# Hybrid block on one core: the weights' second parts made by ScalarE and an accumulating DMA, used last in each block, and three other jobs moved off GpSimd

## The chip, the core and the metric

The kernel runs on one core of a Trainium2 chip. The metric is the device time of one execution in microseconds (us). Three runs of the kernel before gave 914.47, 915.35 and 921.18 us; the median, 915.35 us, is the time that the change is compared with.

## The reference: what is computed

One layer over 512 tokens of width 1024, all in float32:

```python
h = rmsnorm(x, attn_norm_g)
proj = h @ w_in                                   # 1024 x 5408
p_sb, p_rw, p_gate = jnp.split(proj, ...)
# A: stick-breaking attention, 8 heads of 64, swept in blocks of 128 queries
# B: RWKV-7 time mixing, 8 heads of 64: state update over 512 steps, group norm, bonus, gate
gates = jax.nn.sigmoid(p_gate + branch_gate_b)
x = x + (sum over branches of gates * (branch @ w_branch)) @ w_out
u_gate, u_val = causal_depthwise_conv(rmsnorm(x) @ w_ffn_up)   # 1024 x 5632
x = x + (silu(u_gate) * u_val) @ w_ffn_down                    # 2816 x 1024
```

## The kernel before

Everything is kept transposed: channels on the 128 partitions, the 512 tokens along the free dimension. A dense product is cut into **blocks** of 128 output channels. Each operand of a block is split into two parts of a shorter format: `hi` is the rounded value, and `lo` is what the rounding left over. A block of 1024 input channels is then 8 k-steps of three matmuls, 24 in all: `hi` of the weight with `hi` of the activation (line 127), `hi` of the weight with `lo` of the activation (line 128), and `lo` of the weight with `hi` of the activation (line 129).

The weight of a block goes through four steps, in `load_w` and `load_w2`: SP's queue issues the load of `wraw` (512 KB); ScalarE (ACT) rounds it to `whi`; a subtraction `wraw - whi` gives `wlo`, in two halves of four k-steps each; TensorE (PE) uses both. `wraw` and `whi` have two buffers, `wlo` four halves, so two blocks are in hand. The subtraction is on VectorE (DVE), but while `state["pool"]` is set, which is in the whole first phase, it is on GpSimd (POOL).

The program has two phases. In **phase 1** (to about 450 us) PE serves several streams at once: `dense_stream` makes the projection's blocks (tiles `pd`), four `rw_stream`s make the RWKV branch (tiles `pr`), four `att_stream`s the attention (tiles `pz`, `po`). `interleave` merges them: each stream yields what its matmuls cost, or how long it has to wait, and a table of latencies (`LAT`) says how far ahead dense work is put. That order is fixed when the program is built; the order on the other engines is set by a list scheduler, and every engine then works strictly in its own order. In **phase 2** (gates, branches, output, feed-forward) there are dense blocks alone, on tiles `pf`; there the subtraction is on DVE before and after the change.

In phase 1 the dense stream calls `load_w(..., half=True)` for the next block when it starts a block: that issues the load, the rounding, and the first half of `wlo`. The second half follows after the fourth k-step of the running block.

Of the other streams three places matter. `rw_stream` prepares for each pair of heads the tiles `ARV` and `BK`: the values are copied into `ARV` by POOL (line 435), and each of the two products that fill `BK` (lines 448 and 453) is made half by DVE and half by POOL. The next step (line 456, DVE) overwrites an input of the second product, so it waits for POOL's half. `L517` and `L519` are the 31 steps of a triangular solve, two short DVE instructions each. `att_stream` makes for each piece of scores a softmax-like chain: three ACT steps on `e`, one on DVE (line 701), a split into `sph` (ACT, line 121) and `spl` (DVE, line 122), two matmuls into `pz`, two ACT steps for `w`, and a DVE step `wtl` (line 733); POOL keeps the running sums (`e`, `ach`, `acl`, lines 709 to 712).

Of the kernel before, what the change touches and what calls it, by code (L numbers as in the profile page):

```python
# [12 lines left out]
ALU = mybir.AluOpType  # L13
# [3 lines left out]
P = 128  # L17
D = 1024
T = 512
KT = D // P  # L20
# [32 lines left out]
def hybrid_block(ctx: ExitStack, tc: tile.TileContext, xT, w_in, vecs, decay_up, iclr_up, out_gate_up,  # L53
                 w_branch, w_out, w_up, w_down, out):
    nc = tc.nc
    V, A, G, PE = nc.vector, nc.scalar, nc.gpsimd, nc.tensor
# [3 lines left out]
    state = {"load": None, "members": [], "funcs": ()}  # L60
# [17 lines left out]
    def f(ap):  # L78
        return ap.bitcast(F32)
# [16 lines left out]
        return vec[:, o : o + w] if o < NVEC1 else state["vec2"][:, o - NVEC1 : o - NVEC1 + w]  # L96


    def load_w(src, nk, half=False):


        raw = wpool.tile([P, KT, P], F32, tag="wraw", name="wraw")
        nc.sync.dma_start(raw[:, 0:nk], src.rearrange("(k p) c -> p k c", p=P))
        hi = wpool.tile([P, KT, P], F32R, tag="whi", name="whi")
        A.copy(hi[:, 0:nk], raw[:, 0:nk])  # L105
        w = (hi, [], raw)
        for _ in range(1 if half or nk <= 4 else 2):
            load_w2(w, nk)
        return w

    def load_w2(w, nk=KT):
        hi, los, raw = w
        k0 = 4 * len(los)
        n = min(4, nk - k0)
        lo = wpool.tile([P, 4, P], F32R, tag="wlo", name="wlo", bufs=4)
        (G if state.get("pool") else V).tensor_tensor(lo[:, 0:n], raw[:, k0 : k0 + n], f(hi[:, k0 : k0 + n]),  # L116
                                                      op=ALU.subtract)
        los.append(lo)

    def split(hi, lo, src):  # L120
# [3 lines left out]
    def mm1(ps, w, k, act, first, last):  # L124

        (ah, al), hi, lo = act, w[0][:, k], w[1][k // 4][:, k % 4]
        PE.matmul(ps, hi, ah, start=first, stop=False)  # L127
        PE.matmul(ps, hi, al, start=False, stop=False)  # L128
        PE.matmul(ps, lo, ah, start=False, stop=last)  # L129
# [11 lines left out]
    h_acts = [(hhi[:, k], hlo[:, k]) for k in range(KT)]  # L141
# [32 lines left out]
    gl1 = cpool.tile([96, T], F32R, name="gl1")  # L174
# [18 lines left out]
    with tc.tile_pool(name="p0", bufs=1) as p0, \  # L193
# [39 lines left out]
        for k in range(KT):  # L233
# [6 lines left out]
                PE.matmul(ps, w[1][k // 4][:, k % 4], hhi[:, k], start=False, stop=False)  # L240
            for ps, w in (pl0, w0), (pk0, w1):
                PE.matmul(ps, w[0][:, k], hlo[:, k], start=False, stop=(k == KT - 1))
        state["pool"] = True
        mu1 = cpool.tile([P, 15], F32, name="mu1")
        V.tensor_scalar(mu1, vcol("mu", 0, 15), -1.0, 1.0, op0=ALU.mult, op1=ALU.add)
        ndb = cpool.tile([P, 8], F32, name="ndb")
# [10 lines left out]
        for j in range(2):  # L257
            hr = slice(64 * j, 64 * j + 64)
# [76 lines left out]
    def c3(a):  # L335
        return a.rearrange("p (c t) -> p c t", t=CH)
# [43 lines left out]
    def rw_stream(p):  # L380
        d = RD[p]
# [6 lines left out]
        for j, bn in ((0, "db"), (1, "ib")):  # L388
            pl = rbank()
            PE.matmul(pl, lup[j][:, p * P : (p + 1) * P], wl2[j], start=True, stop=False)  # L390
            hr = slice(64 * j, 64 * j + 64)
# [40 lines left out]
        r = d["r"]  # L432
        ARV = rwp.tile([P, NC, 3, CH], F32, tag="ARV", name="ARV", bufs=2)
        for h, (hr, _) in enumerate(HROWS):
            G.tensor_copy(ARV[hr, :, 2 - h, :], c3(d["v"])[hr])
        BK = rwp.tile([P, NC, 2, CH], F32, tag="BK", name="BK", bufs=1)
        Rp = ARV[:, :, 0, :]
        act(c, c, AF.Exp, scale=GAM)
# [4 lines left out]
        for h, (hr, _) in enumerate(HROWS):  # L443
            V.scalar_tensor_tensor(ARV[hr, :, 1 + h, :], c3(kk)[hr], -1.0, c3(c)[hr], op0=ALU.mult, op1=ALU.mult)
        V.tensor_tensor(kk, kk, ic, op=ALU.mult)
        for E, h in (V, 0), (G, 1):
            hr = HROWS[h][0]
            E.tensor_tensor(BK[hr, :, h, :], c3(kk)[hr], e3[hr], op=ALU.mult)
        V.tensor_scalar(ic, ic, vcol("keya", p), ka1[:, p : p + 1], op0=ALU.mult, op1=ALU.add)
        V.tensor_tensor(k, k, ic, op=ALU.mult)  # L450
        for E, h in (V, 0), (G, 1):
            hr = HROWS[h][0]
            E.tensor_tensor(BK[hr, :, 1 - h, :], c3(k)[hr], e3[hr], op=ALU.mult)
        V.tensor_tensor(Rp, Rp, c3(r), op=ALU.mult)

        V.scalar_tensor_tensor(k, r, vcol("rk", p), k, op0=ALU.mult, op1=ALU.mult)
# [330 lines left out]
    def load_gl(c0):  # L787

        raw = wpool.tile([P, KT, P], F32, tag="wraw", name="wraw")
        nc.sync.dma_start(raw[:, :, 0:32], w_in[:, c0 : c0 + 32].rearrange("(k p) c -> p k c", p=P))  # L790
        hi = wpool.tile([P, KT, P], F32R, tag="whi", name="whi")
        A.copy(hi[:, :, 0:32], raw[:, :, 0:32])
        G.tensor_tensor(hi[:, :, 32:64], raw[:, :, 0:32], f(hi[:, :, 0:32]), op=ALU.subtract)
        return hi, None, raw

    def dense_stream():
# [27 lines left out]
        while cur:  # L824
            c0, evac, args, name, gate_ev = cur
            for e in gate_ev:
                yield ("after", e)
            yield ("after", f"bank{i - 2}")
            w, cur = nxt, pick()
            if cur:  # L830
                nxt = load_gl(cur[0]) if cur[3] == "gl1" else load_w(w_in[:, cur[0] : cur[0] + P], KT, half=True)
            ps = bank()
            for k in range(KT):
                if name == "gl1":
                    PE.matmul(ps[0:64], w[0][:, k, 0:64], hhi[:, k], start=(k == 0), stop=False, skip_group_check=True)
                    PE.matmul(ps[0:32], w[0][:, k, 0:32], hlo[:, k], start=False, stop=(k == KT - 1),
                              skip_group_check=True)
                else:
                    mm1(ps, w, k, h_acts[k], k == 0, k == KT - 1)
                if k == 3 and cur and nxt[1]:  # L840
                    load_w2(nxt)
                yield (435 if name == "gl1" else 665, 0)
            evac(*args, ps)
            yield ("set", name, LAT["evac"])
            yield ("set", f"bank{i}", LAT["evac"])
            i += 1
# [63 lines left out]

    interleave([rw_stream(p) for p in range(4)] + [chain(*(att_stream(p) for p in range(4))), dense_stream()])
    ph1.close()
    state["pool"] = False


    load_set(SET_SG, (AF.Sigmoid, AF.Tanh))
# [144 lines left out]
```

## Time and the profile before

| | |
|---|---|
| median of three runs | 915.35 us |
| the profiled execution, its own time | 918.29 us |
| its span, first to last instruction | 916.5 us |
| phase 1 after the prologue, 40 to 450 us: PE busy | 380.74 of 410 us |
| the same stretch: DVE, ACT, POOL busy | 285.97, 258.04, 179.45 us |
| phase 2, 450 to 916 us: PE busy | 462.81 of 466 us |

The profile is of one execution, 1.8 us longer than its span, and 2.9 us longer than the median of the runs. A busy time counts the time in which an engine runs at least one instruction; waits for a semaphore and the issue of a DMA are not in it. A wait is put down to the instruction that ended it.

### The profile page before, as it was taken

What the parts mean: (1) busy time and instruction counts of PE and PEld (TensorE: products, weight loads), DVE (VectorE), ACT (ScalarE), POOL (GpSimd) and SP (SyncE); (2) the same over time, 40 slices, a digit from 0 to 9 for tenths busy, and PEclk for the clock granted to TensorE, in tenths of its full rate; (3) what the DMA queues carried; (4) which work ended last, traced back from release to release, by engine and by line L of the source; (5) the groups of instructions that cost most, each with busy time, mean ns of one, the idle gap of its engine ahead of it and who ended that gap; (6) DMA issues with size and microseconds to landing.
All of it is one profiled execution on the core that took longest, in us unless ns stands there. A gap on an engine that the chain in (4) does not pass through costs nothing.

```text
span 916.5 us, 12769 instructions
## 1 busy us (share of the span) xinstructions
PE 869.6 (95%) x4722; PEld 673.6 (73%) x4722; DVE 581.5 (63%) x1096; ACT 468.2 (51%) x818; POOL 194.0 (21%) x216
## 2 busy tenths in 40 slices
PE   4898888998989998999999999999999999999998
PEld 2665665666767766777788888888888888888886
DVE  5566698796698679254665556777777777632322
ACT  6566756754764666468655445444444444312111
POOL 2463563525535444433000000000000000000000
PEclk8997999998999999999999999999999999999999
DMA  7221213313323321521655543333333333233331
GB/s 208 67 69 51 65 46 71 81 48 86 87 58 71 88 62 54 137 81 36 207 176 149 149 127 92 93 92 102 105 92 92 93 106 100 86 116 108 112 113 41
DMA packets 164479, 87.54 MB, mean 96 GB/s; under 512 B 28384, under 2 KB 155488, under 8 KB 164416
## 3 DMA queue, kind: packets, MB, share of 16 engines
q1 hardware_dynamic: 161392, 81.61, 31.6%
q10 hardware_dynamic: 3024, 5.11, 1.6%
q8 instruction: 37, 0.61, 0.3%
q14 instruction: 26, 0.21, 0.1%
HBM read 78.31 MB, written 8.39 MB: 95 GB/s over the span
## 4 chain that ended last, share of the span: by engine, by line
PE 64%; DVE 5%; ACT 2%; issue 1%; POOL 1%; DVEq 0%; ACTq 0%; POOLq 0%
PE pf L127 17%; PE pf L128 17%; PE pf L129 17%; PE pd L127 3%; PE pd L129 2%; PE pd L128 2%; DVE U L519 1%; DVE tm L517 1%; ACT e L69 1%; DVE spl L122 1%; POOL wlo L116 0%; PE pr L587 0%; DVE wtl L733 0%; PE pz L694 0%; PE pz L727 0%
## 5 line engine op out<-in xcount | busy, mean ns | idle before, releaser
L105 ACT CAST whi<-wraw 128x1024 fp32r<-128x1024 f32 (+1 forms) x132 | 130.1, 985 | 181.2 <-PE pf L128 144.0
L116 DVE TENSOR_TENSOR wlo<-wraw,whi 128x512 fp32r<-128x512 f32 (+1 forms) x178 | 113.7, 676 | 81.8 <-ACT whi L105 79.6
L127 PE MATMUL pf<-h2h,whi 128*128 128x512 f32 x352 | 137.3, 390 | 0.0
L128 PE MATMUL pf<-h2l,whi 128*128 128x512 f32 x352 | 136.9, 389 | 0.0
L129 PE MATMUL pf<-h2h,wlo 128*128 128x512 f32 x352 | 136.9, 389 | 0.0
L127 PE MATMUL pd<-hhi,whi 128*128 128x512 f32 x296 | 127.6, 431 | 3.8 <-ACT whi L105 1.8
L116 POOL TENSOR_TENSOR wlo<-wraw,whi 128x512 fp32r<-128x512 f32 x74 | 101.4, 1391 | 120.0 <-ACT whi L105 105.5
L129 PE MATMUL pd<-hhi,wlo 128*128 128x512 f32 x296 | 120.1, 406 | 1.5 <-POOL wlo L116 1.5
L128 PE MATMUL pd<-hlo,whi 128*128 128x512 f32 x296 | 119.8, 405 | 0.0
L127 PEld LDWEIGHTS pf<-h2h,whi 128*128 128x128 f32 x352 | 66.1, 188 | 14.1 <-issue 0.2
L128 PEld LDWEIGHTS pf<-h2l,whi 128*128 128x128 f32 x352 | 66.1, 188 | 13.8 <-issue 0.2
L129 PEld LDWEIGHTS pf<-h2h,wlo 128*128 128x128 f32 x352 | 66.1, 188 | 13.7
L127 PEld LDWEIGHTS pd<-hhi,whi 128*128 128x128 f32 x296 | 57.0, 193 | 19.6 <-ACT whi L105 2.5
L129 PE MATMUL pf<-dh,wlo 128*128 128x512 f32 x176 | 69.3, 394 | 0.0
L127 PE MATMUL pf<-dh,whi 128*128 128x512 f32 x176 | 69.3, 394 | 0.0
L128 PE MATMUL pf<-dl,whi 128*128 128x512 f32 x176 | 69.3, 394 | 0.0
L129 PEld LDWEIGHTS pd<-hhi,wlo 128*128 128x128 f32 x296 | 57.2, 193 | 15.5 <-POOL wlo L116 2.8
L128 PEld LDWEIGHTS pd<-hlo,whi 128*128 128x128 f32 x296 | 57.1, 193 | 9.6 <-issue 0.5
L1000 DVE TENSOR_TENSOR u<-pf,rs 128x512 f32<-128x512 f32 x44 | 30.3, 688 | 38.7 <-PE pf L129 38.6
L121 ACT CAST dh<-cv 128x512 fp32r<-128x512 f32 x22 | 13.7, 621 | 62.0 <-DVE cv L1009 62.0
L519 DVE TENSOR_TENSOR U<-U,tm 128x60 f32<-128x60 f32 (+24 forms) x124 | 43.3, 350 | 2.0
L129 PEld LDWEIGHTS pf<-dh,wlo 128*128 128x128 f32 x176 | 32.9, 187 | 8.3
(304 smaller groups left out, 1636.3 us busy)
## 6 DMA issues: line engine op xcount, KB each, us to landing
wraw<-in_w_up SPq DMA_DIRECT2D x44, 512.0 KB, 3.7
wraw<-in_w_in SPq DMA_DIRECT2D x42, 512.0 KB, 3.7
wraw<-in_w_down SPq DMA_DIRECT2D x16, 512.0 KB, 4.1
wraw<-in_w_branch SPq DMA_DIRECT2D x16, 256.0 KB, 2.8
wraw<-in_w_out SPq DMA_DIRECT2D x8, 512.0 KB, 4.1
gd<-gs ACTq DMA_DIRECT2D x13, 256.0 KB, 2.0
g<-gd SPq DMA_DIRECT2D x13, 256.0 KB, 2.8
wraw<-in_w_down SPq DMA_DIRECT2D x8, 384.0 KB, 3.4
```

The lines of the kernel that those rows point to most:

```text
L69: ins = A.activation(o, i, func, **kw)
L105: A.copy(hi[:, 0:nk], raw[:, 0:nk])
L116: (G if state.get("pool") else V).tensor_tensor(lo[:, 0:n], raw[:, k0 : k0 + n], f(hi[:, k0 : k0 + n]), op=ALU.subtract)
L121: A.copy(hi, src)
L122: V.tensor_tensor(lo, src, f(hi), op=ALU.subtract)
L127: PE.matmul(ps, hi, ah, start=first, stop=False)
L128: PE.matmul(ps, hi, al, start=False, stop=False)
L129: PE.matmul(ps, lo, ah, start=False, stop=last)
L517: V.tensor_tensor(tv, U[:, 0:m, q : q + 1].broadcast_to([P, m, n]), N[:, q : q + 1, q + 1 :].broadcast_to([P, m, n]), op=ALU.mult)
L519: V.tensor_tensor(U[:, 0:m, q + 1 :], U[:, 0:m, q + 1 :], tv, op=ALU.add)
L1000: V.tensor_tensor(u, ps, rs2, op=ALU.mult)
```

## The change

In phase 1 the subtraction `wraw - whi` is no longer an instruction of POOL. ACT writes `-whi` into `wlo` (one ACT instruction for each half), and POOL's queue issues a DMA that adds `wraw` to it (`accum_op=ALU.add`), 256 KB a time. Both halves are now requested together when `load_w` is called, and the block's matmuls are put in another order: first the 16 with `whi`, then the 8 with `wlo`. The copies of the values into `ARV` go from POOL to ACT, and POOL's halves of the two `BK` products to DVE. The scratch for descriptors of POOL's DMAs goes from 1024 to 4096 bytes of a partition. `state["pool"]` is renamed `state["dma"]`.

```diff
-    def load_w(src, nk, half=False):
+    def load_w(src, nk):
...
-        for _ in range(1 if half or nk <= 4 else 2):
+        for _ in range(1 if nk <= 4 else 2):
             load_w2(w, nk)
...
         lo = wpool.tile([P, 4, P], F32R, tag="wlo", name="wlo", bufs=4)
-        (G if state.get("pool") else V).tensor_tensor(lo[:, 0:n], raw[:, k0 : k0 + n], f(hi[:, k0 : k0 + n]),
-                                                      op=ALU.subtract)
+        if state.get("dma"):
+
+            A.mul(lo[:, 0:n], f(hi[:, k0 : k0 + n]), -1.0)
+            G.dma_start(lo[:, 0:n], raw[:, k0 : k0 + n], accum_op=ALU.add)
+        else:
+            V.tensor_tensor(lo[:, 0:n], raw[:, k0 : k0 + n], f(hi[:, k0 : k0 + n]), op=ALU.subtract)
...
         for h, (hr, _) in enumerate(HROWS):
-            G.tensor_copy(ARV[hr, :, 2 - h, :], c3(d["v"])[hr])
+            A.copy(ARV[hr, :, 2 - h, :], c3(d["v"])[hr])
...
-        for E, h in (V, 0), (G, 1):
+        for h in range(2):
             hr = HROWS[h][0]
-            E.tensor_tensor(BK[hr, :, h, :], c3(kk)[hr], e3[hr], op=ALU.mult)
+            V.tensor_tensor(BK[hr, :, h, :], c3(kk)[hr], e3[hr], op=ALU.mult)
...
-        for E, h in (V, 0), (G, 1):
+        for h in range(2):
             hr = HROWS[h][0]
-            E.tensor_tensor(BK[hr, :, 1 - h, :], c3(k)[hr], e3[hr], op=ALU.mult)
+            V.tensor_tensor(BK[hr, :, 1 - h, :], c3(k)[hr], e3[hr], op=ALU.mult)
...
-                nxt = load_gl(cur[0]) if cur[3] == "gl1" else load_w(w_in[:, cur[0] : cur[0] + P], KT, half=True)
+                nxt = load_gl(cur[0]) if cur[3] == "gl1" else load_w(w_in[:, cur[0] : cur[0] + P], KT)
...
-                else:
-                    mm1(ps, w, k, h_acts[k], k == 0, k == KT - 1)
-                if k == 3 and cur and nxt[1]:
-                    load_w2(nxt)
-                yield (435 if name == "gl1" else 665, 0)
+                    yield (435, 0)
+            else:
+
+                todo = [(w[0][:, k], a) for k in range(KT) for a in h_acts[k]]
+                todo += [(w[1][k // 4][:, k % 4], h_acts[k][0]) for k in range(KT)]
+                for n, (w_, a) in enumerate(todo):
+                    PE.matmul(ps, w_, a, start=(n == 0), stop=(n == len(todo) - 1))
+                    if n % 3 == 2:
+                        yield (665, 0)
...
-    nc = bacc.Bacc("TRN2", target_bir_lowering=False, num_devices=1, dynamic_dma_scratch_size=1024)
+    nc = bacc.Bacc("TRN2", target_bir_lowering=False, num_devices=1, dynamic_dma_scratch_size=4096)
```

The lines of `hybrid_block` behind the change stand three further down (L701 becomes L704); the matmuls of a dense block in phase 1 are all on L847, the rounding is L104, the negation L117, the DMA L118.

Three places show what moves. The first is PE's own row of instructions in the first dense block of phase 1, where the block meets the first short-rank matmuls of the RWKV stream (`lup`); before:

```order
L129 MATMUL pd<-hhi,wlo 128x512
L127 MATMUL pd<-hhi,whi 128x512
L390 MATMUL pr<-wl_0_80,lup_78 128x512
L392 MATMUL pr<-wl_90,lup_78 128x512
L128 MATMUL pd<-hlo,whi 128x512
L129 MATMUL pd<-hhi,wlo 128x512
```

and after, at the same place:

```order
L847 MATMUL pd<-hhi,whi 128x512
L847 MATMUL pd<-hlo,whi 128x512
L393 MATMUL pr<-wl_0_80,lup_78 128x512
L847 MATMUL pd<-hhi,wlo 128x512
L395 MATMUL pr<-wl_90,lup_78 128x512
L847 MATMUL pd<-hhi,wlo 128x512 x7
L393 MATMUL pr<-wl_1_81,lup_79 128x512
```

Before, every third matmul of a block read `wlo`; now its 16 matmuls with `whi` are through before the first with `wlo`, and the other streams' matmuls stand at nearly the same places between them.

The second is ACT's row at the start of the first attention, where `e` is the softmax-like chain; before:

```order
L69 ACTIVATE e_896<-pz_892 128x128
L69 ACTIVATE e_909<-pz_905 128x256
L69 ACTIVATE e_896<-e_896 128x128
L69 ACTIVATE e_909<-e_909 128x256
L69 ACTIVATE e_896<-e_896 128x128
L69 ACTIVATE e_909<-e_909 128x256
L69 ACTIVATE t1_846<-t1_846 128x512
L121 CAST sph3_901<-e_896 128x128
```

and after:

```order
L104 CAST whi_898<-wraw_896 128x1024
L69 ACTIVATE e_914<-pz_910 128x128
L117 ACTIVATE wlo_900<-whi_898 128x512
L117 ACTIVATE wlo_903<-whi_898 128x512
L69 ACTIVATE e_914<-e_914 128x128
L69 ACTIVATE e_927<-pz_923 128x256
L69 ACTIVATE e_914<-e_914 128x128
L69 ACTIVATE e_927<-e_927 128x256
L104 CAST whi_1019<-wraw_1017 128x1024
L124 CAST sph3_919<-e_914 128x128
```

The two negations of a block now stand between the steps of that chain.

The third is POOL's row in the same attention, where `e`, `ach`, `acl` are its running sums; before:

```order
L116 TENSOR_TENSOR wlo<-wraw,whi 128x512 x2
L709 TENSOR_TENSOR e<-e 128x128
L711 CAST ach<-e 128x256
L712 TENSOR_TENSOR acl<-e,ach 128x256
L116 TENSOR_TENSOR wlo<-wraw,whi 128x512 x2
L709 TENSOR_TENSOR e<-e 128x256
```

and after:

```order
L118 DMA wlo<-wraw 128x512 x3
L712 TENSOR_TENSOR e<-e 128x128
L118 DMA wlo<-wraw 128x512
L714 CAST ach<-e 128x256
L715 TENSOR_TENSOR acl<-e,ach 128x256
L712 TENSOR_TENSOR e<-e 128x256
```

The subtractions' places in POOL's row are taken by the DMA issues, each of which waits for its negation on ACT.

## Rows read from the trace of the kernel before

**Rows 1.** The page: busy time of each engine over the span (share, instructions).

```profile
PE 869.6 (95%) x4722; PEld 673.6 (73%) x4722; DVE 581.5 (63%) x1096; ACT 468.2 (51%) x818; POOL 194.0 (21%) x216
```

**Rows 2.** Stretches: length; PE, PEld, DVE, ACT, POOL busy (instructions); clock, DMA, GB/s.

```profile
40.00:450.00 410.00, 380.74 (x2637) 280.69 (x2638) 285.97 (x638) 258.04 (x545) 179.45 (x191) 0.97 0.28 74
450.00:916.00 466.00, 462.81 (x2013) 376.83 (x2012) 273.13 (x415) 185.49 (x238) 0.00 (x0) 1.00 0.37 112
...
60.00:80.00 20.00, 16.53 (x72) 12.33 (x72) 14.98 (x18) 10.00 (x18) 9.87 (x6) 0.82 0.19 55
...
120.00:140.00 20.00, 16.81 (x74) 11.63 (x73) 19.94 (x45) 11.21 (x23) 12.62 (x12) 1.00 0.19 53
```

**Rows 3.** Waits of PE, 40 to 460 us: us in total, times, longest.

```profile
PE pz L727 <- DVE spl L122: 4.7, 7, 1.4
PE pr L590 <- DVE Z L606: 2.9, 3, 1.1
PE po L744 <- DVE wtl L733: 2.5, 3, 1.8
PE pr L150 <- ACT slh L121: 2.5, 1, 2.5
PE pr L390 <- DVE rkb L465: 2.2, 1, 2.2
...
PE pd L127 <- ACT whi L105: 0.9, 1, 0.9
PE pd L129 <- POOL wlo L116: 0.9, 2, 0.7
...
PE pd L127 <- DVE xv L164: 0.2, 1, 0.2
```

**Rows 4.** Groups by form, 0 to 470 us: busy, mean ns, then idle before.

```profile
L116 POOL TENSOR_TENSOR wlo<-wraw,whi 128x512 fp32r<-128x512 f32 x74 | 101.4, 1391 | 120.0 <-ACT whi L105 105.5 <-PE pz L696 6.5 <-issue 4.2
...
L435 POOL COPY ARV<-xv 64x512 f32<-64x512 f32 x8 | 10.7, 1332 | 1.1 <-DVE xv L164 0.8
...
L654 DVE TENSOR_TENSOR wtl<-sq,wth 128x512 fp32r<-128x512 f32 x8 | 8.4, 1052 | 18.6 <-ACT sq L69 16.7 <-ACT wth L69 1.8
...
L448 POOL TENSOR_TENSOR BK<-t,t 64x512 f32<-64x512 f32 x4 | 6.9, 1732 | 0.3
...
L456 DVE SCALAR_TENSOR_TENSOR xk<-xr,vec,xk 128x512 f32<-128x512 f32 x4 | 6.4, 1589 | 3.6 <-POOL BK L453 3.6
...
L733 DVE TENSOR_TENSOR wtl<-w,wth 128x512 fp32r<-128x512 f32 x8 | 5.5, 684 | 0.7 <-ACT w L69 0.7
...
L121 ACT CAST sph<-e 128x512 fp32r<-128x512 f32 x8 | 5.0, 620 | 2.8 <-DVE e L701 2.8
...
L670 ACT CAST k<-rawk 64x512 fp32r<-64x512 f32 x8 | 4.9, 618 | 0.2
...
L448 DVE TENSOR_TENSOR BK<-t,t 64x512 f32<-64x512 f32 x4 | 4.8, 1195 | 0.0
```

**Rows 5.** Timeline near 267 us, POOL and DVE: start, length, instruction.

```profile
266.39 0.22 DVE L517 TENSOR_TENSOR tm<-U,N 128x66 f32<-128x66 f32 x1
...
267.00 1.29 DVE L519 TENSOR_TENSOR U<-U,tm 128x66 f32<-128x66 f32 x1
...
266.88 2.55 POOL L116 TENSOR_TENSOR wlo<-wraw,whi 128x512 fp32r<-128x512 f32 x2 [2.40 <-ACT whi L105]
```

**Rows 6.** Timeline, first dense block of phase 1, ACT and PE.

```profile
32.94 1.04 ACT L105 CAST whi<-wraw 128x1024 fp32r<-128x1024 f32 x1 [4.75 <-PE pr L242]
33.89 0.68 ACT L69 ACTIVATE wal<-pr,mu 128x512 f32<-128x512 f32 x1
34.04 0.50 PE L127 MATMUL pd<-hhi,whi 128*128 128x512 f32 x1 [0.91 <-ACT whi L105]
...
48.13 0.39 PE L127 MATMUL pd<-hhi,whi 128*128 128x512 f32 x1
48.35 0.39 PE L128 MATMUL pd<-hlo,whi 128*128 128x512 f32 x1
```

**Rows 7.** DMA issues: size, median us from issue to landing.

```profile
wraw<-in_w_in SPq DMA_DIRECT2D x42, 512.0 KB, 3.7
...
gd<-gs ACTq DMA_DIRECT2D x13, 256.0 KB, 2.0
...
os<-orw SPq DMA_DIRECT2D x2, 256.0 KB, 4.9
```

More of the change, by code (lines that the diff above doesn't have):

```diff
@@ L242, in hybrid_block @@
                 PE.matmul(ps, w[0][:, k], hlo[:, k], start=False, stop=(k == KT - 1))
-        state["pool"] = True
+        state["dma"] = True
         mu1 = cpool.tile([P, 15], F32, name="mu1")
@@ L830, in dense_stream @@
             if cur:
-                nxt = load_gl(cur[0]) if cur[3] == "gl1" else load_w(w_in[:, cur[0] : cur[0] + P], KT, half=True)
+                nxt = load_gl(cur[0]) if cur[3] == "gl1" else load_w(w_in[:, cur[0] : cur[0] + P], KT)
             ps = bank()
-            for k in range(KT):
-                if name == "gl1":
+            if name == "gl1":
+                for k in range(KT):
                     PE.matmul(ps[0:64], w[0][:, k, 0:64], hhi[:, k], start=(k == 0), stop=False, skip_group_check=True)
@@ L912, in hybrid_block @@
     ph1.close()
-    state["pool"] = False
+    state["dma"] = False
     load_set(SET_SG, (AF.Sigmoid, AF.Tanh))
```

## The prediction

> **What bounds the kernel now.** I read the page's busy times first: PE is busy for 95% of the span, so time can only be won where PE waits or runs slowly [rows 1]. The view of stretches says where that is. In phase 2 PE is busy for 462.81 of 466 us at full clock, and the change touches nothing there but line numbers. In phase 1 from 40 to 450 us it is busy for 380.74 of 410 us at a mean granted clock of 0.97 [rows 2]. So two sums are open: about 29 us of waits, and 3% of 410, about 12 us, of lowered clock. The view of PE's waits names what ended them. It has 23 rows, of which the larger and the last are shown: 14 end at DVE (21.8 us together), 8 at ACT (6.8 us) and one at POOL (0.9 us) [rows 3]. POOL's subtraction itself, the thing that the change replaces, is almost never what PE waits for.
>
> Its cost is elsewhere. The groups by form show the same DVE instruction on the same shape at two prices: `wtl` takes 684 ns on L733 and 1052 ns on L654, and the three-input step on L456 takes 1589 ns [rows 4]. The timeline shows why: a solve step of 128x66 takes 0.22 us, and its neighbour, begun while POOL runs two subtractions, 1.29 us [rows 5]. A DVE instruction that reads two tiles is held until POOL's instruction is through. DVE is at 285.97 of 410 us, and in one stretch at 19.94 of 20 while PE has 16.81 [rows 2]. ACT has most room: 258.04 of 410.
>
> **The change, part by part.**
>
> *The subtraction leaves POOL.* 74 instructions of 1391 ns, 101.4 us, 37 blocks with two halves each [rows 4]. What DVE gets back lies between 8.6 us, the excess over 684 ns of L654 (8 x 0.37), L456 (4 x 0.9) and DVE's L448 (4 x 0.5) alone, and 96 us, all the time that L116 holds POOL in the stretch. When I set every DVE instruction of the timeline from 20 to 460 us beside the shortest of its form (rows 5 are two of them), the excess is 56 us, and 35 us of it falls into L116's time. I take 35; POOL's `BK` and `ARV` work accounts for another 8. DVE takes over eight half products at 0.68 us, 5.5 us. So DVE falls from 286 to about 248 us. That is an estimate of DVE's time, not of the kernel's.
>
> *What of it reaches PE.* The 21.8 us of waits that end at DVE end chains in which DVE runs two to four instructions beside ACT and PE. Between nothing (the chain is ACT's) and all 21.8 I take half, 11 us: DVE's work shrinks by an eighth, but the largest of these waits lie where it is saturated. The 2.5 us at `slh` and 0.9 us at `wlo` are due to POOL too (L456 stands 3.6 us idle for POOL's half of `BK`, and ACT's `slh` comes behind it) [rows 3, 4]: 2 us of 3.4. The clock is low where PE waited, as in 60 to 80 us (0.82, PE busy 16.53 of 20) [rows 2]; with fewer waits I take back 3 of the 12 us, the bounds being 0 and 12.
>
> *The negations go to ACT.* 74 instructions of the form 128x512, for which ACT's cast of that shape is the row: 620 ns, 46 us; and 8 copies of 64x512 at 618 ns, 5 us [rows 4]. ACT goes from 258 to about 309 of 410 us, from 63% to 75%. Queued behind a negation on ACT are the steps of the attention's chain (the order shows two negations, 1.24 us, between two steps of `e`), the roundings and the `ARV` copies. ACT's idle share shrinks by a third, from 37 to 25%; waits that end at ACT, now 6.8 us, should grow by half: I take +4 us. The lower bound is 0, the upper one 22 us, if in half of the 37 blocks the 1.24 us falls on a chain that PE awaits.
>
> *The accumulating DMA.* No row shows one, nor a DMA issued by POOL. The nearest are 256 KB transfers of the other queues, 2.0 to 4.9 us to landing [rows 7]. An add must also read what it adds to, so I take 4 us, near the longer end. The Trainium skill (DMA: Bandwidth & Descriptors, Anatomy of one DMA) fits a DMA from GpSimd at about 2.0 us plus bytes over 436e3, 2.6 us for 256 KB; by that estimate the sum below would be 1 us lower. What hides it: PE's matmuls of 512 columns follow each other at 0.23 us (48.13 to 48.35) [rows 6], so a block takes 5.5 us alone, and its 16 matmuls with `whi` 3.7 us. The slot for block i+1 is free at the end of block i-1, so negation and landing have 9.2 us even where nothing stands between the blocks, and in most places 10 to 15. Two negations and 4 us fit, with the queue on ACT. If that cover is gone, every microsecond beyond it is PE's. It is gone in the first block: `whi` is ready at 33.98, ACT evacuates `wal` (0.68) and negates twice, so the first half is asked for near 35.2 and lands at 37.2 to 40.1, while PE, started at 34.04, wants it at 37.7 [rows 6]. That is 0 to 2.4 us for this block, and the second half comes after it: +2 us.
>
> *POOL's queue.* Before, POOL stood 105.5 us waiting for `whi` with the running sums behind it [rows 4]; now it waits for the negations in the same places. The issue itself costs POOL less than the 1391 ns of the subtraction, or about as much, so I put it at nothing. SP's loads of `wraw` now wait for an accumulating DMA to land, where they waited for a subtraction; the slot is needed a block later, so that is hidden by that block. The order of matmuls within a block costs nothing: the same 24.
>
> Sum: -11 - 2 - 3 + 4 + 2 = **-10 us**. Against the profiled execution that is 916.5 - 10 in the span, 918.29 - 10 in its own time; that execution is 2.9 us over the median, so against the median 915.35 - 10 = **905 us**.
>
> **The rivals.**
>
> 1. *ACT takes DVE's place (slower).* Every engine works in its built order, so the negations delay what is behind them whether or not PE is in a hurry for `wlo`. At the upper bound, 22 us, against the gain of 16, and the first block's 2, the kernel ends 8 us later: 923 us. For it: the order puts them inside the `e` chain. Against: ACT has 8 to 10 us idle in the DVE-bound stretches (11.21 busy of 20 at 120 us). It decides from about 20 us of PE waits that end at ACT.
> 2. *The accumulating DMA is late everywhere (slower).* If the second half lands more than 9.2 us after the slot is free, the dense stretches stall. The order has about 12 blocks with nothing between; at 12 us each loses 3 us, 36 us: with the gain 915 + 36 - 16 = 935 us. For it: 28% of the DMA engines' time is already used in the stretch, and 19 MB more have to be read, added and written. Against: the longest 256 KB row is 4.9 us. The Trainium skill (DMA: Bandwidth & Descriptors, Issuing engines are not separate DMA queues) says that DMAs of all queues run on the same 16 engines and interleave, which is the way in which the loads' 3.7 us would grow too; no run here shows it yet.
> 3. *The waits only move (no change).* PE's order and the latencies planned into it stay; DVE's freed time lies where PE was filled with dense blocks anyway, so 6 or 7 us come back and ACT and the first block take 6: 914 us.
> 4. *The relief reaches nearly everything.* All of the waits at DVE and half of the clock: -22 - 3 - 6 + 4 + 2, 890 us.
>
> **How the numbers follow.** A measurement of this kernel tells about 1%, 9 us, from no change. Chances: forecast 0.40, rival 3 0.27, rival 1 0.15, rival 2 0.07, rival 4 0.11. The forecast lies at the edge of 1%, from 897 to 912 by its bounds, so 0.30 of its 0.40 count as faster; with rival 4 and a little of rival 3, faster by over 1%: 0.43; within 1%: 0.37; slower: 0.20. The range runs from 891 to 923: it leaves out rival 2, the worse half of rival 1 and the better half of rival 4.
>
> **What would show it.** Right: the mean of `wtl` on the old L654 falls towards 684 ns and DVE's busy time in the stretch to about 250 us; PE's waits at DVE fall to about 11 us; ACT's busy time rises by some 50 us and PE's waits at ACT to 10 or 11; the accumulating DMA lands in about 4 us and PE waits for it in the first blocks only. Rival 1 shows as waits at ACT above 20 us. Rival 2 shows as waits of matmuls with `wlo` for a DMA in the middle of the phase. Wrong altogether if DVE's instructions stay as long as they are, because POOL holds DVE while it issues DMAs.

## The result and the profile after

The changed kernel took **907.08 us** (median of 4 runs, 905.56 to 908.80) beside 918.26 us for the kernel before on the same chip: ratio **0.989**, 95% interval 0.985 to 0.994. In a later comparison it was 905.45 against 915.12 us (0.988, 0.984 to 0.993). The forecast was 905 us from 915.35, so both the sign and the size hold; the profiled execution took 908.44 us, with a span of 906.6. One run of a later kernel, `c_order_only`, lies 1.7% above that kernel's fastest and is left out of its mean as slow. What follows shows that the sum came out right although two of its terms did not.

The page's busy times, beside [rows 1]:

```profile
PE 864.9 (95%) x4722; PEld 668.4 (74%) x4722; DVE 544.6 (60%) x1104; ACT 508.0 (56%) x900; POOL 129.9 (14%) x200
```

The two stretches (length; PE, PEld, DVE, ACT, POOL busy; clock, DMA share, GB/s), beside [rows 2]:

```profile
40.00:450.00 410.00, 385.38 (x2679) 282.96 (x2678) 257.76 (x656) 305.07 (x637) 118.49 (x174) 0.98 0.58 128
450.00:906.00 456.00, 452.50 (x1969) 368.46 (x1967) 266.32 (x405) 178.03 (x226) 0.00 (x0) 1.00 0.36 107
```

DVE has 28 us less in the stretch, ACT 47 us more, POOL 61 us less, and the DMA engines' share went from 0.28 to 0.58. The first matmul of the branches in phase 2 (`pf` from `oh`) starts at 443.81 us, where it started at 454.13: the 10 us come from the time before it alone.

PE's waits from 40 to 460 us (total, times, longest), beside [rows 3]. All 19 rows make 24.3 us, where the 23 of before made 29.5: 7.5 at DVE, 10.2 at ACT, 6.6 at DMAs.

```profile
PE pr L543 <- DMA U<-st: 4.1, 3, 2.5
PE pr L484 <- ACT QA L496: 3.3, 2, 2.1
PE pd L847 <- ACT gs L785: 2.8, 1, 2.8
PE pd L847 <- DMA wlo<-wraw: 2.5, 5, 1.1
PE pd L847 <- DVE gy L167: 2.1, 1, 2.1
PE pz L727 <- DVE tm L520: 1.8, 2, 1.2
```

The groups by form, 0 to 470 us, that answer to [rows 4] (busy, mean ns, then idle before and what ended it):

```profile
L118 POOL DMA_DIRECT2D wlo<-wraw x74 | 65.1, 912 | 191.6 <-ACT wlo L117 111.8 <-PE pd L847 17.4 <-ACT e L69 9.5
...
L657 DVE TENSOR_TENSOR wtl<-sq,wth 128x512 fp32r<-128x512 f32 x8 | 5.9, 734 | 28.5 <-ACT sq L69 24.9 <-ACT wth L69 3.6
...
L451 DVE TENSOR_TENSOR BK<-t,t 64x512 f32<-64x512 f32 x8 | 5.5, 685 | 0.2
...
L459 DVE SCALAR_TENSOR_TENSOR xk<-xr,vec,xk 128x512 f32<-128x512 f32 x4 | 3.0, 746 | 0.0
...
L117 ACT ACTIVATE wlo<-whi 128x512 fp32r<-128x512 f32 x74 | 45.5, 630 | 1.9 <-ACT QA L598 0.7 <-ACT gs L785 0.4 <-ACT Y L616 0.3
L104 ACT CAST whi<-wraw 128x1024 fp32r<-128x1024 f32 x39 | 40.8, 1047 | 45.8 <-DMA wraw<-in_w_in 25.0 <-PE pd L847 8.0 <-PE pr L554 5.5
...
L438 ACT COPY ARV<-xv 64x512 f32<-64x512 f32 x8 | 4.9, 612 | 0.0
```

The cast of the raw weights in the same view of the kernel before:

```profile
L105 ACT CAST whi<-wraw 128x1024 fp32r<-128x1024 f32 x39 | 40.8, 1047 | 35.9 <-PE pd L128 13.6 <-issue 5.2 <-PE pr L242 4.7
```

The page's row of the accumulating DMAs (size, median us from issue to landing), for [rows 7]:

```profile
wlo<-wraw POOLq DMA_DIRECT2D x74, 256.0 KB, 3.9
```

Three things are to be seen. DVE's held instructions are short again: 1052 ns became 734, 1589 became 746, 1195 became 685. The accumulating DMA lands in 3.9 us, and POOL spends 912 ns on each issue. And one wait is new: before, the largest waits of ACT's cast of the raw weights ended at PE, and none at its load; now it stands 25.0 us idle for the load of `wraw`.

### The profile page after: what moved, and what is told of

It reads as the page before. It is cut to its first block, busy times and chain, and to the rows that moved or that the text cites. A ratio compares the mean times of both kernels' runs of the same rounds, so it can differ in the third digit from the quotient of the medians.

```text
span 906.6 us, 12925 instructions
## 1 busy us (share of the span) xinstructions
PE 864.9 (95%) x4722; PEld 668.4 (74%) x4722; DVE 544.6 (60%) x1104; ACT 508.0 (56%) x900; POOL 129.9 (14%) x200
## 4 chain that ended last, share of the span: by engine, by line
PE 80%; ACT 6%; DVE 5%; DMA 5%; issue 2%; SPq 1%; POOL 1%; POOLq 0%; ACTq 0%
PE pf L130 17%; PE pf L131 17%; PE pf L132 17%; PE pd L847 15%; DMA wraw<-in_w_in 2%; DMA wlo<-wraw 1%; DVE tm L520 1%; SPq L529 1%; ACT whi L104 1%; PE pz L730 1%; PE pr L603 1%; PE pr L489 1%; PE pr L590 1%; ACT wlo L117 1%; ACT t L69 1%
## 5 line engine op out<-in xcount | busy, mean ns | idle before, releaser
L104 ACT CAST whi<-wraw 128x1024 fp32r<-128x1024 f32 (+1 forms) x132 | 130.0, 985 | 192.6 <-PE pf L131 143.6
L847 PE MATMUL pd<-hhi,whi 128*128 128x512 f32 x296 | 122.8, 415 | 6.5 <-ACT gs L785 2.8
L847 PE MATMUL pd<-hlo,whi 128*128 128x512 f32 x296 | 121.8, 411 | 0.0
L118 POOL DMA_DIRECT2D wlo<-wraw x74 | 65.1, 912 | 191.6 <-ACT wlo L117 111.8
L847 PE MATMUL pd<-hhi,wlo 128*128 128x512 f32 x296 | 86.0, 409 | 2.8 <-DMA wlo<-wraw 2.7
L132 PEld LDWEIGHTS pf<-h2h,wlo 128*128 128x128 f32 x352 | 66.1, 188 | 13.8
L130 PEld LDWEIGHTS pf<-h2h,whi 128*128 128x128 f32 x352 | 66.1, 188 | 13.8 <-issue 0.2
L847 PEld LDWEIGHTS pd<-hhi,whi 128*128 128x128 f32 x296 | 56.8, 192 | 20.5 <-ACT gs L785 3.3
L847 PEld LDWEIGHTS pd<-hhi,wlo 128*128 128x128 f32 x296 | 53.6, 190 | 17.4 <-DMA wlo<-wraw 5.9
L847 PEld LDWEIGHTS pd<-hlo,whi 128*128 128x128 f32 x296 | 56.8, 192 | 11.7 <-issue 0.5
L117 ACT ACTIVATE wlo<-whi 128x512 fp32r<-128x512 f32 x74 | 45.5, 630 | 1.9 <-ACT QA L598 0.7
L130 PEld LDWEIGHTS pf<-dh,whi 128*128 128x128 f32 x176 | 32.9, 187 | 8.3
```

The lines of the kernel that those rows point to most:

```text
L117: A.mul(lo[:, 0:n], f(hi[:, k0 : k0 + n]), -1.0)
L118: G.dma_start(lo[:, 0:n], raw[:, k0 : k0 + n], accum_op=ALU.add)
L847: PE.matmul(ps, w_, a, start=(n == 0), stop=(n == len(todo) - 1))
```

## The experiments

Two sums are used for all of them. **DVE's excess** sets each DVE instruction that has a row of its own in the timeline from 20 to 460 us beside the shortest of its form: 59.7 us before (the prediction's count of the same trace said 56), 17.9 after. With the instructions that the timeline merges into one row counted as well it is 61.2 and 19.2. And since every run lists its span and mean granted clock, each span splits into **span x clock**, the span had the clock been full, and the rest, which is what the clock took at most (a low clock costs nothing while PE idles). Means over each kernel's runs in us, and both parts against the kernel before on the same chip:

```
kernel          runs  ratio   95% interval      span  clock  span x clock      the rest
before (chip 2)  29                            915.6  0.982  899.1             16.5
a_dma_only        6   0.985  0.981 to 0.988    901.8  0.993  895.3  ( -3.8)     6.5  (-10.0)
b_bkv_only       12   0.993  0.991 to 0.996    908.6  0.985  895.1  ( -4.0)    13.6  ( -2.9)
c_order_only     11   0.992  0.989 to 0.995    907.9  0.986  894.9  ( -4.2)    13.0  ( -3.5)
d_dma_mixed      12   0.996  0.993 to 0.998    912.5  0.981  894.9  ( -4.2)    17.6  ( +1.1)
before (chip 10) 19                            915.4  0.981  898.2             17.2
e_pool_reads      4   1.041  1.039 to 1.044    951.5  0.963  915.8  (+17.6)    35.7  (+18.5)
f_pool_writes     5   1.005  1.002 to 1.007    918.5  0.976  896.7  ( -1.5)    21.9  ( +4.7)
k_order_mid       9   0.993  0.991 to 0.995    908.1  0.985  894.6  ( -3.6)    13.5  ( -3.7)
j_a_one          10   0.993  0.990 to 0.996    908.2  0.982  891.6  ( -6.6)    16.6  ( -0.6)
before (chip 13)  7                            914.6  0.983  899.1             15.4
m_raw3            4   0.976  0.970 to 0.981    892.4  0.992  885.0  (-14.1)     7.4  ( -8.0)
n_pool_again      4   1.016  1.010 to 1.022    929.4  0.976  907.1  ( +8.0)    22.3  ( +6.9)
p_after_again     4   0.988  0.984 to 0.993    903.7  0.986  891.3  ( -7.8)    12.4  ( -3.0)
before (chip 5)  11                            915.1  0.981  898.0             17.1
q_raw3_all        6   0.977  0.974 to 0.980    893.6  0.989  883.6  (-14.4)    10.0  ( -7.1)
```

The first theory was the prediction's: POOL's subtraction held DVE, and its leaving shortens the chains that PE waits for. The rivals were the new order of the matmuls (the second theory), the move of `B`, `K` and `V` (the third), and a gain that is only the clock's.

**The parts one by one.** First the accumulating DMAs with their new order, without the third edit:

```diff
-            A.copy(ARV[hr, :, 2 - h, :], c3(d["v"])[hr])
+            G.tensor_copy(ARV[hr, :, 2 - h, :], c3(d["v"])[hr])
...
-        for h in range(2):
+        for E, h in (V, 0), (G, 1):
```

> The changed kernel with the copies of V and the halves of B and K put back on GpSimd: only the weights' second parts and their order are changed. If the gain comes from GpSimd's subtractions no longer holding VectorE (first theory), most of it stays: ratio to the kernel before about 0.991, VectorE's busy time from 40 to 450 us near 262 us instead of 286. If the gain is that of the B, K and V work (third theory), the ratio is 1.00.

Measured: 0.985, DVE's excess 24.6, PE's waits 21.2 us (8.1 at DVE, 10.6 at ACT, 2.5 at DMAs). The first two edits carry the whole gain in time. But 10.0 us of it are clock: at full clock they gain 3.8 us, where the changed kernel, on another chip, gains 7.8. Then the third edit alone, on the kernel before:

> The kernel before with only the copies of V moved to ScalarE and the halves of B and K to VectorE; the subtraction stays on GpSimd. First theory: VectorE is still held by 74 subtractions, so at most 3 us come back, ratio 0.997 to 1.00. Third theory: the ratio is 0.99.

Measured: 0.993, PE's waits 26.4 us (13.8 at DVE, 11.5 at ACT). The excess is 52.8 in the rows alone, but 60.5 against 61.2 with the merged ones, so DVE is hardly relieved. The edit pays by itself, yet added to the first two it shortens the time no further. Then the order alone, with POOL's subtraction kept:

```diff
-                    mm1(ps, w, k, h_acts[k], k == 0, k == KT - 1)
...
+                todo = [(w[0][:, k], a) for k in range(KT) for a in h_acts[k]]
+                todo += [(w[1][k // 4][:, k % 4], h_acts[k][0]) for k in range(KT)]
```

> The kernel before with only the order of matmuls in a block changed (16 with the first parts, then 8 with the second parts) and both halves of the subtraction requested at the block's start, still on GpSimd. If using the second parts last is what pays (second theory), the ratio is 0.99, since TensorE no longer meets a second part that has only just been made. First theory: TensorE waited 0.9 us for it in all, so the ratio is 0.998 to 1.002 and VectorE's instructions stay as long as before.

Measured: 0.992, with the excess (59.0) and PE's waits (28.2 us) as before. So the kernel with the order alone is faster too, and not by freeing DVE; how much of that is the order's own is taken up below. And the accumulating DMAs with the old order:

> The changed kernel with the old order of matmuls in a block, so that the third matmul of a block reads the second part that the accumulating DMA makes. The cover falls from 9.2 us (a block and 16 matmuls) to about 5.5 us (a block), the negations and a landing of 3.9 us need about 6: first theory expects TensorE to wait for the DMA some 5 to 15 us in all, ratio 0.995 to 1.005. If the order doesn't matter, the ratio is that of the changed kernel, 0.989.

Measured: 0.996. DVE is relieved as in the changed kernel (excess 19.1, 4.4 us of waits at DVE), but PE waits 15.9 us for DMAs. The first row of its view of PE's waits is the cost:

```profile
PE pd L848 <- DMA wlo<-wraw: 12.4, 8, 3.4
```

What DVE gave back went to transfers that landed too late for the interleaved order. Using the second parts last cuts this wait from 12.4 to 2.5 us. It does not lower the sum: all of PE's waits make 24.2 us here and 24.3 in the changed kernel, where more of them lie at ACT.

**Why the order pays by itself.** The order edit of before, but with the second half asked for in the middle of the block, as it was:

> The kernel before with only the order of the 24 matmuls changed (those with the second parts last); the second half of the second parts is still asked for in the middle of the block before. It splits the run in which order and request were changed together (0.992). Theory (the order itself pays, since the second parts are then needed 3.7 us later): 0.990 to 0.995. Rival 1 (the early request paid): 0.998 to 1.002. Rival 2 (what that run won was its clock, and the clock goes its own way with every shift of the program): anything from 0.990 to 1.003, with the same waits and the clock's loss as the difference.

Measured: 0.993, as with both requests early; the early request is worth nothing measurable. PE's waits in 40 to 460 us make 27.0 us (16.9 at DVE and 10.1 at ACT, where before had 21.8 and 6.8), and the excess is 57.2; half of the 7 us that this kernel gains is clock.

How much of this is the order's own stays open. In the profiled executions, about half of the lead of both kernels with the order alone arises in one place, and other edits win as much there. PE's 1000th to 1130th matmul take 19.5 us in the kernel before (217.0 to 236.5 us), 15.7 and 14.6 us with the order alone, 14.8 with the third edit alone, and 14.7 with the DMAs in the old order. In the kernel before PE waits there for `vt`, and then the clock is low for 6.8 us; the others have at most 0.95 us of that wait and a full clock. The wait, and two stretches of the kernel before (columns as above):

```profile
PE pr L481 <- DVE vt L685: 1.8, 1, 1.8
...
220.00:225.00 5.00, 3.90 (x30) 2.58 (x30) 2.27 (x7) 3.82 (x10) 0.54 (x4) 0.81 0.52 88
225.00:230.00 5.00, 5.00 (x26) 3.95 (x23) 2.52 (x5) 2.22 (x7) 3.54 (x6) 0.51 0.43 83
```

So 4 to 5 us come back with whichever edit moves that one wait. The order's kernels win another 3 to 4 us between 78 and 98 us, which the third edit alone does not, and lose 2.6 to 2.7 again between 360 and 385; what causes these two the runs don't settle.

**Giving the hold-up back.** The first attempt put a subtraction that nothing depends on behind each issue on POOL:

```diff
+            G.tensor_tensor(dmy[1], dmy[0], dmy[0], op=ALU.subtract)
```

> The changed kernel, and behind each of the 74 accumulating DMAs POOL subtracts a tile of zeros of 128x512 from itself, a result that nothing uses. Theory (POOL's subtraction held DVE, and its leaving is a part of the gain): DVE's excess over the shortest of each form, 18 us in the changed kernel, goes back to 40 or more, PE's waits that end at DVE rise from 7.5 to 12 us or more, and the ratio to before is 0.993 to 1.000. Rival (the gain is the new order of the matmuls and POOL's freed queue; DVE's hold-up cost nothing): DVE's excess comes back but the ratio stays at 0.986 to 0.991.

Its control only wrote:

```diff
+            for _ in range(3):
+                G.memset(dmy[1], 0.0)
```

> The control to the one before: the changed kernel, and behind each accumulating DMA POOL fills a tile of 128x512 three times with zeros, some 1.6 us in which POOL is busy and reads nothing. Theory (it is POOL's reading of tiles that holds DVE): DVE's excess stays below 25 us and the ratio at 0.986 to 0.993. Rival (a busy POOL holds DVE whatever it does, or delays the DMAs behind it): DVE's excess or PE's waits for the DMAs rise as with the subtraction, and the ratio is within 0.002 of that kernel's.

Neither did what it was meant to do. What depends on nothing is put early by the list scheduler, and POOL ran the added work in a heap. The stretch 0 to 40 us of the first (columns as above; POOL's is the fifth busy time):

```profile
0.00:40.00 40.00, 21.04 (x49) 12.14 (x50) 28.48 (x42) 17.94 (x28) 37.83 (x43) 0.82 0.45 130
```

PE's waits from 10 to 40 us in the same kernel:

```profile
PE pr L245 <- ACT hhi L242: 6.0, 1, 6.0
PE pr L248 <- POOL hlo L243: 4.9, 2, 2.7
```

And the first row of its view from 40 to 460 us:

```profile
PE pd L850 <- DMA wlo<-wraw: 27.9, 5, 11.6
```

POOL is full (37.83 of 40) from the start, and the input's second parts `hlo` queue behind the dummies; after 40 us the issues of the accumulating DMAs do, and that is the larger part of the 1.041. The dummies were through by 120 us, so DVE's excess over the whole phase (24.7) hardly moved. The writes (1.005, excess 20.0, 8.2 us of PE's waits at the DMA) were moved up too, and ended near 200 us. So the ratios of these two runs say nothing on the hold-up.

Their traces do, one instruction at a time. Of the DVE instructions of the operations with two input tiles, the 31 that overlap a dummy subtraction have 0.36 us of excess each, as the 88 that overlap POOL's subtraction in the kernel before have 0.41. The 206 that overlap a dummy write have 0.05, and those that overlap neither 0.03 to 0.04. So it is POOL's subtraction that holds DVE, and not a busy POOL. The second attempt ties the extra work to the data, so that it stands where the old subtraction stood:

```diff
+            G.tensor_tensor(dmy[:, 0:n], raw[:, k0 : k0 + n], f(hi[:, k0 : k0 + n]), op=ALU.subtract)
```

> The changed kernel, and POOL subtracts each half of the weights as before as well, into a tile that nothing reads (74 more POOL instructions of some 1.4 us that wait for the cast, as the old ones did). It does what the run with the zeros was meant to do, at the old places. Theory (POOL's subtraction held DVE, and its leaving is a part of the gain): DVE's excess over the shortest of each form, 18 us in the changed kernel, is 45 or more, PE's waits that end at DVE rise from 7.5 to 12 us or more, and the ratio is 0.994 to 1.003. Rival (the hold-up cost PE nothing): the excess comes back, but PE's waits at DVE stay below 10 us and the ratio at 0.986 to 0.993; what rises then is only the wait for the DMAs, which POOL asks for 1 to 2 us later.

Measured: 1.016, 25 us above the changed kernel. DVE's excess is back at 51.0 us. PE's waits at DVE are 20.1 us in 19, where the changed kernel on that chip has 7.3 in 10 and the kernel before had 21.8; those at ACT (10.0 against 9.3) and at DMAs (6.7 against 5.1) hardly differ. The first of its waits of PE that end at DVE:

```profile
PE pz L733 <- DVE spl L128: 5.6, 5, 2.1
PE pz L730 <- DVE tm L523: 3.7, 2, 2.7
```

And the group of `wtl` in it:

```profile
L660 DVE TENSOR_TENSOR wtl<-sq,wth 128x512 fp32r<-128x512 f32 x8 | 6.5, 811 | 30.5 <-ACT sq L69 24.5 <-ACT wth L69 6.0
```

The wait at `spl` that headed [rows 3] is back, and `wtl` is long again. The 91 DVE instructions that overlap it have 0.38 us of excess each. This confirms the mechanism: it takes about 13 us of PE's waits, and the clock takes 10 us more than in the changed kernel. The ratio lies beyond the range given for it: the costs of the change (16.7 us of waits at ACT and DMAs, where the kernel before had 7.7 at ACT and POOL) stay while its relief is gone. The Trainium skill (SBUF — State Buffer, 🔬 SBUF: two separate sides) describes an exclusive lock between a DVE instruction with two SBUF inputs and a GpSimd instruction that reads SBUF; the excess of 60, 18 and 51 us in three kernels agrees. That POOL does not hold DVE while it only issues DMAs is the trace's: 74 issues of 912 ns, and the 116 DVE instructions of the same kind that overlap one have 1.4 us of excess in all.

**A larger transfer.** On the kernel with the first two edits, one negation and one DMA of 512 KB for a block:

```diff
+            lo = wpool.tile([P, KT, P], F32R, tag="wlo8", name="wlo8")
+            A.mul(lo, f(hi), -1.0)
+            G.dma_start(lo, raw, accum_op=ALU.add)
```

> The changed kernel with B, K and V's copies back on POOL (0.985 in the first call), and one negation and one accumulating DMA of 512 KB for a block in place of two of 256 KB. Theory (the fixed parts count: 37 issues of 0.9 us less on POOL, and 37 fixed parts of a negation less on ACT; the landing of 5 to 7 us still lies behind 16 matmuls and the block before): ratio 0.980 to 0.985. Rival (the longer landing shows: the first matmul with a second part waits for all 512 KB): PE's waits for DMAs rise from 2.5 to 8 us or more and the ratio is 0.986 to 0.993.

Measured: 0.993; PE's waits for the DMA are 3.3 us, so the rival's mechanism is absent, and at full clock it gains 6.6 us, where two halves gained 3.8. But the clock took 16.6 us instead of 6.5. Neither theory had that; why this kernel's clock falls more often is not settled.

**Where 10 us were still lost.** Set beside the kernel before by the starts of the same DVE instructions, the changed kernel is 19 us ahead at 365 us of before, and only 9 to 10 ahead from 380 us on. The timeline there in the changed kernel, SP's queue, ACT and PE (start, length, instruction, idle before):

```profile
349.10 0.59 SPq L527 DMA_DIRECT2D su<-U  x1
349.80 9.60 SPq L529 DMA_DIRECT2D st<-N  x4
359.57 0.50 SPq L102 DMA_DIRECT2D wraw<-in_w_in  x1
...
363.85 1.04 ACT L104 CAST whi<-wraw 128x1024 fp32r<-128x1024 f32 x1 [9.81 <-DMA wraw<-in_w_in]
364.92 0.63 ACT L117 ACTIVATE wlo<-whi 128x512 fp32r<-128x512 f32 x1
365.46 0.57 ACT L785 COPY gs<-pd 128x512 f32<-128x512 f32 x1
...
366.08 0.79 PE L847 MATMUL pd<-hhi,whi 128*128 128x512 f32 x1 [2.84 <-ACT gs L785]
```

Two stretches of it (columns as above):

```profile
360.00:365.00 5.00, 3.24 (x15) 2.35 (x13) 0.00 (x0) 1.12 (x2) 0.00 (x0) 1.00 0.70 147
365.00:370.00 5.00, 3.92 (x10) 3.13 (x11) 0.00 (x0) 3.90 (x7) 2.10 (x3) 0.66 1.02 241
```

Read upwards: PE stands 2.84 us for the evacuation `gs`, and then runs its next matmuls at a lowered clock (0.66 in 365 to 370 us). `gs` stands in ACT's order behind a cast, and that cast 9.81 us for its load. The load was issued at 359.57, behind four small stores of the solve that held SP's queue for 9.60 us. In the kernel before the same four took 4.21 us (timeline, SP's queue):

```profile
367.94 0.59 SPq L524 DMA_DIRECT2D su<-U  x1
368.65 4.21 SPq L526 DMA_DIRECT2D st<-N  x4
```

The stores of all four pairs of heads together: 17.0 us before, 30.6 after, and 16.6 with the third edit alone, which adds no DMA. The stores are long where the accumulating DMAs are. They are not all of it. SP's loads also wait for a free buffer: 240.6 us in 32 waits for `wlo<-wraw` (SP's queue, 40 to 460 us), where before they waited 83.4 us for POOL's `wlo` and 146.9 us for ACT's `whi`. And the kernels with the order alone, which have no such DMA, lose some 3 us at about the same place, so not all 9 us need be the load's.

The experiment asks for each load one block earlier, into a third buffer, on the kernel with the first two edits:

```diff
-        raw = wpool.tile([P, KT, P], F32, tag="wraw", name="wraw")
+        raw = wpool.tile([P, KT, P], F32, tag="wraw", name="wraw", bufs=3)
...
+                    raw2 = load_gl(c1) if c1 == LR0 + 2 * P else load_raw(w_in[:, c1 : c1 + P], KT)
```

> The changed kernel with B, K and V's copies back on POOL (0.985 in the first call), with a third buffer for the raw weights, each of them asked for one block earlier on SP's queue. Theory (the accumulating DMAs crowd the solve's small stores, so SP's queue stands longer at them and the next block's raw weights are asked for late; ACT then waits 27 us for raw weights, and the evacuation behind that cast holds PE): ACT's waits for raw weights fall below 8 us, the 2.9 us of PE at the gate's evacuation vanish, and the ratio to before is 0.974 to 0.982. Rival (those waits of ACT lie beside PE's full queue, or the load is slow and not late): 0.983 to 0.988, as without the third buffer.

> The changed kernel once more, so that it stands beside the third buffer's kernel on the same chip. All theories: 0.985 to 0.993, as in the first comparison; it should show ACT's 25 us of waits for raw weights again, and its clock shows how much that differs from run to run.

Measured on one chip: **893.49 us, 0.976**, against 905.45 us and 0.988 for the changed kernel; the kernel with the first two edits, on which it is built, had 0.985 on another chip. ACT's waits for raw weights fall to 9.3 us, PE's to 14.5 us in all, and the wait for `gs` is gone. In the new kernel's timeline these stores are about as long as before it, and ACT still waits long at one load:

```profile
339.67 9.31 SPq L537 DMA_DIRECT2D st<-N  x4
349.15 0.52 SPq L105 DMA_DIRECT2D wraw<-in_w_in  x1
...
357.61 1.05 ACT L112 CAST whi<-wraw 128x1024 fp32r<-128x1024 f32 x1 [8.78 <-DMA wraw<-in_w_in]
```

The largest of PE's waits in that kernel, and the one behind this cast:

```profile
PE pz L735 <- POOL acl L723: 5.1, 2, 4.7
...
PE pd L865 <- ACT rawq L365: 1.3, 1, 1.3
```

So the earlier load hardly shortens the queue (26.1 us for all four pairs); it takes the block out of its way. ACT's 9.3 us are a little over the 8 expected, and cost PE 1.3 us: `rawq` stands behind the late cast at 358 us as `gs` did. The run changes the number of buffers and the place of the loads in SP's queue together, so it doesn't say which of the two pays. What is left is a running sum on POOL behind POOL's half of `K`. That led to the last run, the third edit on top:

> The changed kernel whole (B, K and V's copies off POOL) with the third buffer for the raw weights, each asked for one block earlier. With the copies and halves still on POOL the third buffer gave 0.976, and there PE waited 4.7 us in one place for POOL's running sum, which stood behind POOL's half of the K product and itself took 3.44 us. Theory (that third edit pays where the loads are no longer late): the wait for POOL falls below 1 us and the ratio is 0.970 to 0.975. Rival (the 4.7 us come back as waits for DVE, which takes the halves over, and for ACT, which takes the copies): PE's waits at DVE and ACT rise from 7.1 to 11 us or more, ratio 0.975 to 0.981.

Measured: 895.13 us, 0.977 (0.974 to 0.980). The wait for POOL is gone, as the theory said, but another came, and it is not the rival's, whose waits at DVE and ACT are 6.9 us together. The first of PE's waits:

```profile
PE pr L551 <- DMA U<-st: 5.1, 2, 2.6
```

PE now waits for the solve's reload behind those same stores. The third edit makes no measurable difference with or without the third buffer. Both kernels with three buffers are ahead of both with two (0.976 and 0.977 against 0.985 and 0.988); which of the two is better, the intervals don't tell.

## Why the prediction was right, and where its steps were not

- **POOL's subtraction holds DVE**: right. Of the excess 35 us were to go with the subtraction and 8 with `BK` and `ARV`; it fell from 59.7 to 24.6 with the first two edits and to 17.9 with all. DVE's busy time in the stretch is 257.8 us and not 248; the stretch now ends 6 us into the branches, which is 2.4 us of that. `wtl` came to 734 ns and not quite to 684.
- **What of it reaches PE, -11 us**: right in kind, and a little small: the waits at DVE went from 21.8 to 7.5 us, and were 20.1 when POOL's subtraction was put back.
- **`slh` and `wlo`, -2 us**: right, and a little small: no wait at `slh` is left (3.2 us before, 2.5 of them named), nor the 0.9 us at POOL's `wlo`. The 2.5 us at the DMA's `wlo` belong to the term for the first blocks.
- **The clock, -3 us with bounds 0 and 12**: -3.0 us in the changed kernel, but -10 with the first two edits and -0.6 with the larger transfer. It is the least predictable term: kernels within 4 us of each other at full clock differ by 10 us by it.
- **ACT, +4 us**: measured 6.8 to 10.2 us. The size held, though without the 3.2 us at `slh` the other waits at ACT grew by 6.6; the reason held only in part: the longest, 2.8 us at `gs`, comes from a late load and not from a negation.
- **The accumulating DMA**: 4 us were taken, 3.9 measured; the estimate by the Trainium skill (DMA: Bandwidth & Descriptors, Anatomy of one DMA), 2.6 us, was too short for a transfer that also adds. PE's waits for it are 2.5 us in 5, all before 70 us: the first blocks, and +2 us, as said. The cover held, and with the old order the same wait was 12.4 us.
- **POOL's issue at nothing**: 912 ns, under the 1391 ns it replaces; no wait of PE ends at POOL.
- **"SP's loads of `wraw` ... hidden by that block"**: the step that failed. The landing of the DMA was considered, and not what 19 MB more do to the others on the same engines: the median of `gd` went from 2.0 to 3.3 us, the solve's stores from 17.0 to 30.6 us of SP's queue, PE waited 4.1 us at `U<-st`, and ACT 25 us for loads, 9.8 of them behind the stores shown. Asking for the loads earlier gave about 1% of the time: 0.985 became 0.976, and 0.988 became 0.977. The Trainium skill (DMA: Bandwidth & Descriptors, Issuing engines are not separate DMA queues) has DMAs of all queues interleave on the same 16 engines; these longer stores agree with that, and rival 2 looked for it at the wrong transfer.
- **"The order of matmuls within a block costs nothing: the same 24"**: no cost shows. The order alone came out 0.7 to 0.8% faster, twice, of which about half lies where other edits gain as much; the rest, 3 to 4 us, has no known cause.

So the -10 held partly by luck. The relief at DVE was 14.3 us and not 11, and the waits that go back to SP's queue (4.1 us at `U<-st`, 2.8 at `gs`), which the sum had at nothing, took more than that back. PE's waits fell by 5.2 us in all and the clock gave 3.0; the other 2 us or so lie in neither. Rival 3 was refuted by the run that put the subtraction back, rival 2 in its own form by 2.5 us of waits, and rival 1 by 10 us at ACT where it needed 20. Rival 4's time, 890 us, was nearly reached by a kernel changed further, and by another way: the loads, not DVE.

## What to carry to other kernels

When work is moved from an engine to DMAs, the transfers' own landing can be the smaller part of the price (here 2.5 us, against about 1% for the late loads): look at which small transfers share the 16 engines, which queue stands behind them, and what else that queue carries. A wait at one engine's cast can hold an evacuation two instructions behind it, so follow PE's waits upwards through the releaser's own idle time. An added dummy instruction must depend on the data whose place it is to hold, or it runs somewhere else; and before a gain of 1% in a kernel bound by PE is given to a mechanism, the granted clock of every run has to be looked at, and the place where the gain arises: three different edits won the same 4 to 5 us at one wait of the kernel before.

## What the runs showed of the hardware that was not expected

An accumulating DMA of 256 KB within the core's own memory lands in 3.9 us (median), one of 512 KB in 4.9 us; each issue holds POOL for 912 ns (878 ns for 512 KB), so few large ones cost POOL less than many small, though that kernel as a whole was no faster. Four stores of 16 KB held SP's queue for 4.21 us before (DMA share 0.44 in 368 to 373 us) and for 9.60 us beside the accumulating DMAs, where the share was 0.73 and 0.89 in the two halves of 350 to 360 us. And the kernels without added work on POOL, all with the same work on PE, differ in mean granted clock from 0.981 to 0.993, which is 10 us of 900; single executions of the kernel before alone range from 0.976 to 0.989.
